# A hybrid decoder layer on one core: two queues issue the first weight loads, and the gates' columns are cast one place later

## The chip, the cores and the metric

The kernel runs on one core of one Trainium2 chip. The metric is the device time of one execution in microseconds (us); less is better. Before the change the median of three runs is 477.52 us (477.06 to 477.61). The core has a matrix engine (PE), a vector engine (DVE), a scalar engine (ACT), a general engine (POOL) and a small engine (SP) that here only issues transfers (DMAs). Every engine works off its own queue of instructions in order. PE accumulates in a small memory (PSUM); the others work in the on-chip memory (SBUF).

## The reference

One layer of a decoder trunk, on 256 tokens of width 1024, in float32:

```
proj = x @ w_in + b_in          # columns: q,k,v,o,i,f of the mLSTM; q,k,v of the attention; two gates
y_a  = sigmoid(o) * head_norm(mlstm_chunkwise(silu(conv(q)), silu(conv(k)), v, i, f))
y_b  = moba_attention(q_b, k_b, v_b, rel_bias)
mix  = (sigmoid(g_a) * (y_a @ w_a) + sigmoid(g_b) * (y_b @ w_b)) @ w_out
x    = layer_norm(ALPHA * x + mix)
x    = layer_norm(ALPHA * x + (silu(g) * up) @ w_down)      # g, up = conv(x @ w_up)
```

The change touches only how the first product begins: `x @ w_in` for the 1024 columns of `o` and the eight columns of the gates `i` and `f`.

## The kernel before

All weights lie in DRAM as a stack `wst` of chunks of 128 partitions by 2048 numbers (1 MB each), in the order in which PE uses them. Each matrix is held as a sum of two rounded parts: ACT casts a piece of the raw float32 weights to the high part (`wh`, line 94), DVE subtracts it from the raw piece and writes the low part (`wl`, line 95), and PE multiplies three times (high by high, high by low, low by high). The helper for such a pair is `split_into`. The input `x` comes transposed (`xraw`) and is split in the same way (`xth`, `xtl`).

The first four chunks make up the columns of `o`, and they are treated apart from the rest (lines 236 to 284). The inner dimension of 1024 is cut into eight steps k of 128 rows. For every k three groups of columns are needed:

- Columns 0 to 511 come from chunks 0 and 1, which are laid out by rows: a piece is 128 x 512 numbers, 256 KB, the widest. Steps 0 to 3 are in `raw` buffer 0 (`raw_105`), steps 4 to 7 in buffer 1 (`raw_106`). Their split goes to `wh_107`/`wl_108` and, for steps 4 to 7, to the borrowed buffers `yah`/`yal`.
- Columns 512 to 767 are chunk 2, whose raw buffer is the borrowed tile `sgb`; its split is `wh_109`/`wl_110`. A piece is 128 x 256 (128 KB), from step 4 on two steps together (256 KB).
- Columns 768 to 1023 are chunk 3, raw buffer `sigo`, split in `wh_111`/`wl_112`, with pieces like those of chunk 2. The eight columns of the gates (`wif`, 32 KB, loaded by POOL's queue) are split into the last eight of each step's 264 columns, so PE's products of this group need them too.

One loop (lines 246 to 259) issues all these loads on SP's queue, step by step: `xraw` first, then for steps 0 and 1 the order chunk 2, chunk 3, `raw`, later chunk 2, `raw`, chunk 3. After step 3 two small loads follow (`sga`, the biases' row, and `bif`). A second loop (lines 266 to 282) casts and subtracts in nearly the same order: `xraw`, chunk 2, (step 0: the gates' columns `wif`), chunk 3 and `raw` for steps 0 and 1. `step_o` (from line 419) then multiplies, step by step, into six accumulators: `ps_o2a`/`ps_o2b` (chunk 2, two halves of the tokens), `ps_o3a`/`ps_o3b` (chunk 3 and the gates) and `ps_o0a`/`ps_o0b` (the 512 columns). Steps 0 and 1 go in the order o2, o3, o0, the later ones o2, o0, o3. Ahead of it PE runs eight multiplications of zeros, `warm_ps` (line 211).

Every DMA from SP's or ACT's queue signals its landing on one of eight semaphores, named DMAHW0 to DMAHW7 here and called lanes below. The eight are dealt out in turn, and a DMA on a lane waits until the one before it on that lane has landed. Before the change the ninth DMA thus waits for the first, and so on. Which lane a load has is read from the cast that waits for it.

After the four chunks the rest of the program follows in `chunk_order`: for each of four groups the projections `qm`, `qb`, `km`, `kb`, `vm`, `vb`, `ga`, `gb`, then `wa`, `wb`, `wo`, the `up` and `dn` parts of the MLP. Their loads (line 89) come behind the first loop on SP's queue.

Of the kernel before, what the change touches and what calls it, by code (L numbers as in the profile page):

```python
# [21 lines left out]
KT = D // P  # L22
# [50 lines left out]
class Kernel:  # L73
# [115 lines left out]
    def run(self):  # L189
        tc, nc, ctx = self.tc, self.nc, self.ctx  # L190
# [45 lines left out]
        raw = [self.stream.tile([P, 2048], F32, tag="raw", name=f"raw{s}", bufs=3) for s in range(2)]  # L236
# [6 lines left out]
        dma = nc.sync.dma_start  # L243
        cut = [(k // 4, slice(k % 4 * 512, k % 4 * 512 + 512)) for k in range(KT)]
        pieces = {0: 1, 1: 1, 2: 1, 3: 1, 4: 2, 6: 2}
        for k, (s, c) in enumerate(cut):
            dma(xraw[:, k], self.xt_d[:, k])
            for t in (2, 3, s) if k < 2 else (2, s, 3):
                if t == s:
                    dma(raw[s][:, c], self.wst[s, :, c])  # L250
                elif k in pieces:
                    d = slice(k * 256, (k + pieces[k]) * 256)
                    dma(raw[t][:, d], self.wst[t, :, d])
                if t == 3 and k == 0:
                    nc.gpsimd.dma_start(self.wif, self.wif_d)
            if k == 3:

                dma(brow.rearrange("p (a d) -> p a d", a=2), self.rows_d[0:2, :].unsqueeze(0))
                dma(bif, self.bif_d.to_broadcast([P, 8]))
# [5 lines left out]
        v3 = [t.rearrange("p (k f) -> p k f", k=KT) for t in whl[3]]  # L265
        for k, (s, c) in enumerate(cut):
            self.split_into(xth[:, k], xtl[:, k], xraw[:, k])
            if k == 0:
                nc.gpsimd.tensor_copy(self.xfirst, xth[:, 0, 0:P])
            n = pieces.get(k, 0)  # L270
            d = slice(k * 256, (k + n) * 256)
            if n:
                self.split_into(whl[2][0][:, d], whl[2][1][:, d], raw[2][:, d])
            if k >= 2:
                self.split_into(whl[s][0][:, c], whl[s][1][:, c], raw[s][:, c])
            if k == 0:
                self.split_into(v3[0][:, :, 256:264], v3[1][:, :, 256:264], self.wif)
            if n:
                self.split_into(*(t[:, k:k + n, 0:256] for t in v3),
                                raw[3][:, d].rearrange("p (k f) -> p k f", k=n))  # L280
            if k < 2:
                self.split_into(whl[s][0][:, c], whl[s][1][:, c], raw[s][:, c])

# [1076 lines left out]
```

## Time and profile before

| | us |
|---|---|
| median of 3 runs | 477.52 |
| the profiled execution, its own time | 477.09 |
| its span, first to last instruction | 475.4 |
| PE busy in the span | 467.9 |
| DVE busy | 369.1 |
| ACT busy | 311.4 |
| POOL busy | 37.8 |

The profiled execution spends 1.7 us of its time outside the span. All views count microseconds from the start of the span. A row of the timeline has start, duration, engine, line, operation, output and inputs, shape, the count, and in brackets how long the engine sat idle before and what ended that. SPq, ACTq and POOLq are the queues that issue; the duration of a DMA there is that of its issue, not of the transfer. The view of the DMAs lists issues by line, count, size and the time from the start of the issue to the landing, which I call the flight. Line 247 issues `xraw`, 253 the pieces of chunks 2 and 3, 250 those of `raw`.

### The profile page before, as it was taken

The page shows a single profiled execution, that of the slowest core. Times are in us where ns is not written, and L with a number is a line of the kernel's source. Part 1 is how long each engine was busy: PE and PEld are TensorE (multiplying, and loading weights), DVE is VectorE, ACT ScalarE, POOL GpSimd, SP SyncE. Part 2 cuts the span into 40 slices and gives each one's busy share as a digit, 9 for nine tenths or more (in the row PEclk, how much of TensorE's full clock was granted, in tenths as well). Part 3 has the DMA queues.
Part 4 walks back from the last instruction along what each step waited for, and adds up shares of the span by engine and source line. Part 5 has one row for each costly group of instructions (what it writes and reads, how often), then busy time and mean ns, then how long its engine had stood idle before and what let it go on. Part 6 is the DMA issues. An engine that isn't in the chain of part 4 may idle for free.

```text
span 475.4 us, 9500 instructions
## 1 busy us (share of the span) xinstructions
PE 467.9 (98%) x3776; PEld 452.8 (95%) x3776; DVE 369.1 (78%) x649; ACT 311.4 (66%) x544; POOL 37.8 (8%) x73
## 2 busy tenths in 40 slices
PE   8999999999999999999999999999999999999994
PEld 6999999999999999999999999999999989999984
DVE  4786979787778778887685798788887775878876
ACT  6679878677868777968563533676555444556871
POOL 0414711000200020000100001000000000000000
PEclk9999999999999999999999999999999999999998
DMA  7995667934893577466966472874456545565202
GB/s 234 296 331 190 214 227 235 327 110 185 246 306 115 189 235 256 169 209 198 373 228 256 148 295 81 301 240 178 171 206 223 199 176 183 187 214 215 90 0 89
DMA packets 31758, 98.92 MB, mean 208 GB/s; under 512 B 11845, under 2 KB 18129, under 8 KB 22497
## 3 DMA queue, kind: packets, MB, share of 16 engines
q1 hardware_dynamic: 30482, 94.08, 56.8%
q0 software_dynamic: 1232, 4.24, 2.8%
q8 instruction: 29, 0.48, 0.4%
q14 instruction: 15, 0.12, 0.1%
HBM read 94.10 MB, written 4.21 MB: 207 GB/s over the span
## 4 chain that ended last, share of the span: by engine, by line
PE 97%; DMA 1%; DVE 0%; SPq 0%; ACT 0%; DVEq 0%; issue 0%; ACTq 0%
PE ps_up L148 25%; PE ffn L148 13%; PE mix L148 5%; PE ps_ga L148 5%; PE ps_kb L148 5%; PE ps_vm L148 5%; PE ps_vb L148 5%; PE ps_gb L148 5%; PE ps_wb L148 5%; PE ps_qm L148 5%; PE ps_km L148 5%; PE ps_qb L148 5%; PE ps_wa L148 4%; PE ps_o0a L437 1%; PE ps_o0b L437 1%; PE psn L148 1%
## 5 line engine op out<-in xcount | busy, mean ns | idle before, releaser
L95 DVE TENSOR_TENSOR wl<-raw,wh 128x1024 fp32r<-128x1024 f32 (+4 forms) x147 | 180.0, 1261 | 28.7 <-ACT wh L94 26.9
L94 ACT CAST wh<-raw 128x1024 fp32r<-128x1024 f32 (+4 forms) x147 | 151.9, 1078 | 12.3 <-DMA raw<-in_wst_dram 3.8
L148 PE MATMUL ps_up<-x1h,wl 128*128 128x256 f32 x320 | 88.4, 276 | 0.0
L148 PE MATMUL ps_up<-x1l,wh 128*128 128x256 f32 x320 | 88.4, 276 | 0.0
L148 PE MATMUL ps_up<-x1h,wh 128*128 128x256 f32 x320 | 88.4, 276 | 0.0
L148 PEld LDWEIGHTS ps_up<-x1l,wh 128*128 128x128 f32 x320 | 60.1, 188 | 0.3
L148 PEld LDWEIGHTS ps_up<-x1h,wh 128*128 128x128 f32 x320 | 60.1, 188 | 0.3
L148 PEld LDWEIGHTS ps_up<-x1h,wl 128*128 128x128 f32 x320 | 60.1, 188 | 0.0
L1131 DVE SCALAR_TENSOR_TENSOR cu<-ps_up,vec,cu 128x255 f32<-128x255 f32 (+1 forms) x80 | 33.1, 476 | 17.3 <-ACT cu L1127 17.3
L148 PE MATMUL ffn<-wh,hl 128*128 128x512 f32 (+2 forms) x94 | 35.5, 378 | 0.0
L148 PE MATMUL ffn<-wl,hh 128*128 128x512 f32 (+2 forms) x94 | 35.4, 377 | 0.0
L94 ACT CAST hh<-cu 128x256 fp32r<-128x256 f32 x22 | 8.9, 407 | 40.3 <-DVE cu L1142 40.3
L148 PE MATMUL ffn<-wh,hh 128*128 128x512 f32 (+2 forms) x94 | 35.3, 375 | 0.0
L1127 ACT ACTIVATE cu<-ps_up,vec 128x256 f32<-128x256 f32 x40 | 16.7, 469 | 17.2 <-PE ps_up L148 17.2
L148 PEld LDWEIGHTS ffn<-wh,hl 128*128 128x128 f32 x94 | 17.7, 188 | 3.2
L148 PEld LDWEIGHTS ffn<-wl,hh 128*128 128x128 f32 x94 | 17.7, 188 | 3.1
L148 PEld LDWEIGHTS ffn<-wh,hh 128*128 128x128 f32 x94 | 17.7, 188 | 3.1
L1022 POOL TENSOR_TENSOR rs<-rs,mhalf 128x1 f32<-128x1 f32 x3 | 2.1, 701 | 229.9 <-DVE rs L1021 229.9
L148 PE MATMUL ps_ga<-xth,wh 128*128 128x256 f32 x64 | 18.0, 281 | 0.0
L148 PE MATMUL mix<-wh,mgh 128*128 128x256 f32 x64 | 17.9, 279 | 0.0
L148 PE MATMUL mix<-wl,mgh 128*128 128x256 f32 x64 | 17.8, 278 | 0.0
L148 PE MATMUL ps_kb<-xth,wl 128*128 128x256 f32 x64 | 17.7, 277 | 0.0
(348 smaller groups left out, 1475.3 us busy)
## 6 DMA issues: line engine op xcount, KB each, us to landing
raw<-in_wst_dram SPq DMA_DIRECT2D x72, 1024.0 KB, 4.9
raw<-in_wst_dram SPq DMA_DIRECT2D x10, 512.0 KB, 6.5
raw<-in_wst_dram SPq DMA_DIRECT2D x8, 256.0 KB, 4.6
lnrow<-in_rows_dram POOLq DMA_DIRECT2D x4, 512.0 KB, 6.8
flip<-turn SPq DMA_DIRECT2D x8, 192.0 KB, 2.1
lg<-flip SPq DMA_DIRECT2D x32, 48.0 KB, 4.8
xraw<-in_xt_dram SPq DMA_DIRECT2D x8, 128.0 KB, 4.5
toe<-table POOLq DMA_DIRECT2D x4, 256.0 KB, 4.2
```

The source lines that it names most:

```text
L94: self.nc.scalar.copy(wh, raw)
L95: self.nc.vector.tensor_sub(wl, raw, wh.bitcast(F32))
L148: self.nc.tensor.matmul(ps, a[i], b[i], start=start and i == 0, stop=stop and i == 2)
L437: mm(ps[t], x[:, k, t * P:(t + 1) * P], w, start=start and k == 0, stop=stop and k == KT - 1)
L1022: nc.gpsimd.tensor_tensor(st["rs"], st["rs"], self.mhalf[:, 0:1], op=ALU.pow)
L1127: act.activation(cu[:, j, :], ps[:, j, :], AF.Copy, scale=tap(2, j))
L1131: v.scalar_tensor_tensor(cu[:, j, o:], ps[:, j, :S - o], tap(t, j), cu[:, j, o:], op0=ALU.mult, op1=ALU.add)
```

## The change

The eight pieces of `raw`, and the first piece of chunk 2, are issued by ACT's queue and no longer by SP's. A new inner function `rows(k)` issues piece k. Piece 0 is issued in the first loop, so at the very front of ACT's queue, together with the first piece of chunk 2. Piece k + 1 is issued in the second loop, right behind the cast of `xraw` of step k. The gates' columns are split behind chunk 3's first piece and not ahead of it.

```
         cut = [...]
         pieces = {0: 1, 1: 1, 2: 1, 3: 1, 4: 2, 6: 2}
+        def rows(k):
+            if k < KT:
+                s, c = cut[k]
+                nc.scalar.dma_start(raw[s][:, c], self.wst[s, :, c])
+
         for k, (s, c) in enumerate(cut):
             dma(xraw[:, k], self.xt_d[:, k])
-            for t in (2, 3, s) if k < 2 else (2, s, 3):
+            for t in (2, s, 3):
                 if t == s:
-                    dma(raw[s][:, c], self.wst[s, :, c])
+                    if k == 0:
+                        rows(k)
                 elif k in pieces:
                     d = slice(k * 256, (k + pieces[k]) * 256)
-                    dma(raw[t][:, d], self.wst[t, :, d])
+                    q = nc.scalar.dma_start if (t, k) == (2, 0) else dma
+                    q(raw[t][:, d], self.wst[t, :, d])
...
             self.split_into(xth[:, k], xtl[:, k], xraw[:, k])
+            rows(k + 1)
...
-            if k == 0:
-                self.split_into(v3[0][:, :, 256:264], v3[1][:, :, 256:264], self.wif)
             if n:
                 self.split_into(*(t[:, k:k + n, 0:256] for t in v3), ...)
+            if k == 0:
+                self.split_into(v3[0][:, :, 256:264], v3[1][:, :, 256:264], self.wif)
             if k < 2:
                 self.split_into(whl[s][0][:, c], whl[s][1][:, c], raw[s][:, c])
```

The front of ACT's queue before, up to the cast of `xraw` of step 1 (a `CAST` row is the high part of a split; in brackets the lane it waits for; DMASW0 is the lane of `wif`):

```order
L94 ACT_TABLE_LOAD
L94 CAST xth<-xraw 128x256 [waits DMAHW0_49]
L94 CAST wh_109<-sgb 128x256 [waits DMAHW1_49]
L94 CAST wh_111<-wif 128x8x8 [waits DMASW0_49]
L94 CAST wh_111<-sigo 128x256 [waits DMAHW2_49]
L94 CAST wh_107<-raw_105 128x512 [waits DMAHW3_49]
L94 CAST xth<-xraw 128x256 [waits DMAHW4_49]
```

The same place now, up to the third piece of `raw`:

```order
L261 DMA sgb<-in_wst_dram 128x256
L250 DMA raw_105<-in_wst_dram 128x512
L94 ACT_TABLE_LOAD
L94 CAST xth<-xraw 128x256 [waits DMAHW1_49]
L250 DMA raw_105<-in_wst_dram 128x512 [waits DMAHW2_49]
L94 CAST wh_109<-sgb 128x256 [waits DMAHW0_49]
L94 CAST wh_111<-sigo 128x256 [waits DMAHW3_49]
L94 CAST wh_111<-wif 128x8x8 [waits DMASW0_49]
L94 CAST wh_107<-raw_105 128x512
L94 CAST xth<-xraw 128x256 [waits DMAHW4_49]
L250 DMA raw_105<-in_wst_dram 128x512 [waits DMAHW7_49]
```

Two issues now stand ahead of the table load, and piece 1 of `raw` stands ahead of the first cast of chunk 2. The lanes of step 0 are 0 (`sgb`), 1 (`xraw`), 2 (`raw` piece 0) and 3 (`sigo`): the cast of piece 0 needs no wait of its own, since the issue of piece 1, four rows ahead of it, has waited for lane 2 already.

SP's queue before, from its eighth issue on:

```order
L250 DMA raw_105<-in_wst_dram 128x512
L247 DMA xraw<-in_xt_dram 128x256 [waits DMAHW0_49]
L253 DMA sgb<-in_wst_dram 128x256 [waits DMAHW1_49]
L250 DMA raw_105<-in_wst_dram 128x512 [waits DMAHW2_49]
L253 DMA sigo<-in_wst_dram 128x256 [waits DMAHW3_49]
L247 DMA xraw<-in_xt_dram 128x256 [waits DMAHW4_49]
```

SP's queue now, from its sixth issue on:

```order
L253 DMA xraw<-in_xt_dram 128x256
L261 DMA sgb<-in_wst_dram 128x256 [waits DMAHW0_49]
L261 DMA sigo<-in_wst_dram 128x256 [waits DMAHW1_49]
L253 DMA xraw<-in_xt_dram 128x256 [waits DMAHW3_49]
L261 DMA sgb<-in_wst_dram 128x256 [waits DMAHW4_49]
L261 DMA sigo<-in_wst_dram 128x256 [waits DMAHW5_49]
```

The pieces of `raw` are gone from SP's queue, so the pieces of chunks 2 and 3 and of `xraw` follow each other directly, and the load of step 2's chunk 2 waits for the first piece of chunk 2. PE's instructions, and DVE's but for the swapped gates' columns, stand in the same order as before.

## Prediction
> **What bounds the kernel now.** I read the page first: engines, then the chain that ended last.
>
> ```profile
> span 475.4 us, 9500 instructions
> PE 467.9 (98%) x3776; PEld 452.8 (95%) x3776; DVE 369.1 (78%) x649; ACT 311.4 (66%) x544; POOL 37.8 (8%) x73
> PE 97%; DMA 1%; DVE 0%; SPq 0%; ACT 0%; DVEq 0%; issue 0%; ACTq 0%
> ```
>
> PE is the chain: 97% of the span. What stands in the chain besides PE is short, and the change touches one piece of it, the start. So I look at the chain in its first 9 us (start, duration, what).
>
> ```profile
> 0.81 0.37 SPq L247
> 1.23 0.43 SPq L253
> 1.71 0.42 SPq L253
> 2.17 3.91 DMA raw<-in_wst_dram
> 6.09 0.02 issue
> 6.11 0.63 ACT wh L94
> 6.78 0.50 PE ps_o0a L437
> ```
>
> The chain begins with the first three issues on SP, then the flight of the first wide piece (`raw` piece 0): issued at 2.17, landed at 6.08, cast at 6.11, multiplied from 6.78. The timeline shows what PE does around it.
>
> ```profile
> 0.85 3.57 PE L211 MATMUL warm_ps<-const-float32-0.0 128*128 128x512 bf16 x8 [0.85 <-PEq L1349]
> ...
> 4.27 0.43 PE L437 MATMUL ps_o2a<-wh,xth 128*128 128x256 f32 x1
> 4.54 0.28 PE L437 MATMUL ps_o2b<-wh,xth 128*128 128x256 f32 x1
> ...
> 5.95 0.29 PE L437 MATMUL ps_o3b<-wl,xth 128*128 128x264 f32 x1
> 6.78 0.50 PE L437 MATMUL ps_o0a<-wh,xth 128*128 128x512 f32 x1 [0.55 <-ACT wh L94]
> ...
> 8.27 0.28 PE L437 MATMUL ps_o2a<-wh,xth 128*128 128x256 f32 x1
> ...
> 11.06 0.28 PE L437 MATMUL ps_o2a<-wh,xth 128*128 128x256 f32 x1
> ```
>
> Step 0 takes PE from 4.27 to 8.27, 4.00 us. Step 1, 8.27 to 11.06, takes 2.79 us and has no gap. Of the 1.21 us between them, 0.15 is the restart of the first product (the second follows after 0.27 and not after 0.12, the spacing of steady products of this width) and stays; **1.06 us is what an undisturbed step 0 would save**. After 6.78 PE never waits: the chain goes on as PE alone, and the first projection starts at 28.09.
>
> ```profile
> 28.09 5.44 PE ps_qm L148 x48
> 33.54 5.44 PE ps_qb L148 x48
> ```
>
> From there block follows block without a gap, so a shift of the start arrives at the end whole, and nothing behind it takes it up.
>
> **The change part by part.** The first product needs the cast of chunk 2's first piece. Before, ACT and SP did this:
>
> ```profile
> 0.81 1.28 ACT L94 ACT_TABLE_LOAD   x1 [0.81 <-PEq L1349]
> 3.22 0.41 ACT L94 CAST xth<-xraw 128x256 fp32r<-128x256 f32 x1 [1.13 <-DMA xraw<-in_xt_dram]
> 3.81 0.41 ACT L94 CAST wh<-sgb 128x256 fp32r<-128x256 f32 x1 [0.19 <-DMA sgb<-in_wst_dram]
> 4.51 0.25 ACT L94 CAST wh<-wif 128x64 fp32r<-128x64 f32 x1 [0.29 <-DMA wif<-in_wif_dram]
> 4.77 0.41 ACT L94 CAST wh<-sigo 128x256 fp32r<-128x256 f32 x1
> ...
> 2.17 0.44 SPq L250 DMA_DIRECT2D raw<-in_wst_dram  x1
> 6.10 0.33 SPq L253 DMA_DIRECT2D sigo<-in_wst_dram  x1
> ```
>
> Now piece 1 of `raw` is issued by ACT ahead of that cast, and it waits for lane 2, that is for the landing of piece 0. ACT's queue is in order. So **everything behind that issue waits for piece 0 as well**: the casts of chunk 2, chunk 3, the gates and `raw` of step 0, thus DVE's subtractions and PE's first product. A wait that held only the last third of step 0 now holds all of it.
>
> The sum, with L for the landing of piece 0: the issue starts 0.03 behind L (as the cast does before, 6.08 to 6.11), takes 0.33 (SP's issues with a wait ahead of them; ACT has issued no DMA before, so its price is taken from there, bounds 0.33 and 0.44), and the first product follows 0.46 behind the start of the cast (3.81 to 4.27). First product: L + 0.82. Once it starts, the other operands of step 0 are there: the casts of chunk 3, gates and `raw` follow each other at some 0.3 to 0.5 us, ahead of PE's groups. So the 1.06 is saved, and the shift is L + 0.82 - 4.27 - 1.06 = **L - 4.51**. It is zero if piece 0 lands at 4.51, that is 1.57 earlier than before.
>
> How early does it land? Issued second on ACT, at the earliest at 1.23, where SP's second issue stood, instead of 2.17. With the same flight it lands at 5.1, a shift of +0.6. If nothing is gained it lands at 6.1, +1.6. The wider ends: the flight of the half as large first piece of chunk 2 from 1.23 (3.8, a shift of -0.7), and the longest flight of a wide piece in this loop from 2.17 (8.3, +3.8).
>
> ```profile
> sgb<-in_wst_dram SPq DMA_DIRECT2D x1, 128.0 KB, 2.6
> sigo<-in_wst_dram SPq DMA_DIRECT2D x1, 128.0 KB, 3.0
> DMA to landing us min/median/max: 3.9/4.6/6.1
> ```
>
> (The last row is of line 250 alone.) Between them the stretches decide (the last two columns are the DMA engines' busy share and GB/s):
>
> ```profile
> 2.00:3.00 1.00, 1.00 (x4) 0.37 (x3) 0.00 (x0) 0.09 (x1) 0.08 (x1) 1.00 0.80 214
> 3.00:4.00 1.00, 1.00 (x4) 0.24 (x2) 0.34 (x1) 0.59 (x2) 0.00 (x0) 1.00 0.89 252
> 4.00:5.00 1.00, 1.00 (x6) 0.73 (x6) 0.72 (x3) 0.69 (x3) 0.00 (x0) 1.00 0.88 156
> 5.00:6.00 1.00, 1.00 (x9) 0.85 (x7) 0.44 (x2) 0.18 (x1) 0.00 (x0) 1.00 0.95 300
> ```
>
> The DMA engines are 0.80 to 0.95 busy from 2 us on, so it is the transfers and not the issues that take the time, and piece 0 now shares them with the pieces that SP issues meanwhile. I credit half of the 0.94 us of the earlier issue: L = 5.6, **a shift of +1.1 us**.
>
> The Trainium skill, page "DMA: Bandwidth & Descriptors", section "Issuing engines are not separate DMA queues", says that transfers issued by several engines run on the same 16 DMA engines and interleave, which saves the sequencer's issue time alone. The busy shares above agree; by that rule the shift lies toward +1.6, by the issue times alone it would be +0.6.
>
> The other edits. The table load moves behind two issues of about 0.42, to 1.65 to 2.93, and the landing of `xraw` at 3.2 hides it; without that cover it costs what it is late. The gates' cast behind chunk 3's: nothing, since chunk 3's piece was issued at 1.71 with a flight of 3.0, so it landed at 4.7, and its cast at 4.77 did not wait for the gates' cast; both sides within 0.25, that cast's length. Seven more issues on ACT, 0.33 to 0.44 each: 2.3 to 3.1 us in some 18 us, against casts of 1.8 us per step of 2.79; PE's 2.79 hide them. SP loses nine issues and runs ahead; chunk 3's piece of steps 4 and 5, which came latest before PE's need, then comes earlier:
>
> ```profile
> 17.47 0.62 ACT L94 CAST wh<-sigo 128x512 fp32r<-128x512 f32 x1 [1.11 <-DMA sigo<-in_wst_dram]
> 18.74 0.28 PE L437 MATMUL ps_o3a<-wh,xth 128*128 128x264 f32 x1
> ```
>
> The cast ends at 18.09 and PE needs it by 18.74 at the latest, so this was tight, but it held nothing up, and there is nothing to win.
>
> Against its own time the sum is 477.09 + 1.1 = 478.2. That execution lies 0.43 under the median of the runs shown (477.52); the prediction is for a median, **478.6 us**.
>
> **The rivals.**
>
> *Piece 0 lands early (not slower).* Issued side by side with nothing else wide in flight, it flies like chunk 2's first piece: L = 3.8, the shift -0.7, **476.9**. It decides at L = 4.51. For it: the flight of 3.9 includes the queue of three pieces ahead. Against: twice the bytes, and the busy shares. Chance 0.20.
>
> *The queues take turns.* ACT's issues fall between SP's, piece 0 is issued at 2.17 as before and lands at 6.1: +1.6, **479.1**. The change then does not do what it says, and only the wait is left. For it: SP's issues are 0.43 back to back and 0.33 after a wait, as if something behind them set the pace. No run here shows ACT issuing. Chance 0.16. The Trainium skill, same page, section "Queues, rings and completion order", says that SP and ACT have rings of their own but no descriptor generator of their own; that is this case.
>
> *PE runs slowly after the longer pause.* The eight products of zeros take 3.57 us, 0.45 each, where products of the same 512 columns later follow each other after 0.23:
>
> ```profile
> 7.35 0.40 PE L437 MATMUL ps_o0a<-wh,xtl 128*128 128x512 f32 x1
> 7.58 0.40 PE L437 MATMUL ps_o0b<-wh,xtl 128*128 128x512 f32 x1
> ```
>
> The PEclk column reads 1.00 in both, so only the spacing tells. Now PE pauses from 4.42 to 6.4. If it falls back for a stretch of 3.57 at half the pace, that costs 1.8 more: **480.4**. Against: the pause of 0.55 before did nothing, and 2.0 is still short of 3.57. Chance 0.10. The Trainium skill, page "TensorE: Matmul & The Clock Gate", section "What's actually happening", states half the clock until a window of 3413 ns was busy; the spacing agrees, and no run here shows what 2 us of pause do.
>
> *ACT's own loop sets the pace.* A piece of `raw` is issued only behind the next step's `xraw` cast, which stands behind the cast of the piece before. From a landing to the issue two pieces later lie some 1.1 us of casts; with the flight that must fit in two steps, 5.58 us, so flights up to about 4.4 are hidden. Before they were 3.9 to 6.1. At 5.0, piece 1 is 0.4 late (it must land 4.6 behind L) and each of two further rounds 0.6: 1.6 more, **480.2**. Against: ACT's queue holds at most two pieces. Chance 0.12.
>
> **How the numbers follow.** The forecast has 0.42, from +0.6 to +1.6 around 478.6. A measurement of this kernel tells about 0.2% (0.95 us) from no change, so the bound is 478.47; of the forecast I put 0.24 above it and 0.18 below. Slower: 0.24 + 0.16 + 0.10 + 0.12 = 0.62. Faster by that much would need L under 3.56, below the early rival's 3.8: 0.04 of its 0.20. The same: 0.18 + 0.16 = 0.34. The range, 477.1 to 480.6, takes in all but half of the early rival and the worst of the last two.
>
> **What would show it.** ACT's third issue starting within 0.1 us of piece 0's landing, and chunk 2's first cast behind it, not at 3.8: the wait is real. The first product at L + 0.8, then step 0 in about 2.9 us without the gap at 6.2: the 1.06 is saved. The first projection at 29.2 instead of 28.09: the sum. A spacing of 0.2 in the first products of 256 columns would be the slow pace; gaps ahead of `ps_o0a` in steps 1, 3 or 5 ACT's loop. I am wrong if that cast starts before piece 0 has landed, or if the piece lands before 4.5.

## The result and the profile after

The changed kernel takes 480.45 us in the median of eight runs (479.2 to 483.8), the kernel before 477.35 in eight runs beside it (477.06 to 478.23). The ratio is 1.0073, with an interval from 1.006 to 1.0087: slower by 3.1 us. The forecast was 478.6, slower by 1.1; the direction was right and the size was not.

The profiled execution of the changed kernel took 481.24 us, 4.15 more than the one of before (477.09). Its page, with the span, the busy times and the engines' shares of the chain:

```profile
span 479.5 us, 9500 instructions
...
PE 468.5 (98%) x3776; PEld 452.7 (94%) x3776; DVE 368.7 (77%) x649; ACT 310.0 (65%) x544; POOL 36.2 (8%) x73
...
PE 93%; DMA 5%; ACT 1%; DVE 0%; ACTq 0%; DVEq 0%; issue 0%
```

PE is busy for 468.5 us, almost as before (467.9), while the span grew by 4.1: PE waits more. The transfers' share of the chain went from 1% to 5%. The chain of waits of the changed kernel, cut to its first 35 us (start, duration, what), shows for whom it waits:

```profile
0.80 0.41 ACTq L261
...
1.24 4.07 DMA raw<-in_wst_dram
...
5.33 0.33 ACTq L250
...
5.70 1.38 ACT wh L94 x4
...
7.27 3.74 DMA raw<-in_wst_dram
...
11.04 5.87 DMA raw<-in_wst_dram
...
17.29 8.97 DMA raw<-in_wst_dram
...
26.28 0.63 ACT yah L94
...
26.95 0.50 PE ps_o0a L446
```

The first rows are the forecast's path: piece 0 of `raw` is issued at 1.24 and lands at 5.30, the third issue starts 0.03 behind that, and only then come the casts. The row at 17.29 is a second delay, not in the forecast's sum: piece 6 of `raw` flies 8.97 us, and step 6 waits for it. The rows between show why it was issued only then: ACT issues piece 2 at 7.27, piece 4 at 11.04, when piece 2 has landed, and piece 6 at 17.29, when piece 4 has landed (16.91) and its cast has begun. PE's timeline of the changed kernel, the first product of steps 0 to 3 and the one that waits in step 6:

```profile
6.16 0.39 PE L446 MATMUL ps_o2a<-wh,xth 128*128 128x256 f32 x1 [1.75 <-ACT wh L94]
...
9.08 0.28 PE L446 MATMUL ps_o2a<-wh,xth 128*128 128x256 f32 x1
...
11.91 0.28 PE L446 MATMUL ps_o2a<-wh,xth 128*128 128x256 f32 x1
...
15.39 0.28 PE L446 MATMUL ps_o2a<-wh,xth 128*128 128x256 f32 x1
...
26.95 0.50 PE L446 MATMUL ps_o0a<-yah,xth 128*128 128x512 f32 x1 [2.28 <-ACT yah L94]
```

Step 1 starts at 9.08 instead of 8.27 (+0.81). Step 2, from 11.91 to 15.39, takes 3.48 us instead of 2.79 (+0.69). In step 6 PE stands still for 2.28 us, and the step takes 5.36 instead of 2.84 (+2.5). Together 4.0, which is the growth of the span. So three delays have to be explained, and only the first was in the forecast.

### The profile page after: what moved, and what is told of

It reads as the page before. It is cut to its first block, busy times and chain, and to the rows that moved or that the text cites. A ratio compares the mean times of both kernels' runs of the same rounds, so it can differ in the third digit from the quotient of the medians.

```text
span 479.5 us, 9500 instructions
## 1 busy us (share of the span) xinstructions
PE 468.5 (98%) x3776; PEld 452.7 (94%) x3776; DVE 368.7 (77%) x649; ACT 310.0 (65%) x544; POOL 36.2 (8%) x73
## 4 chain that ended last, share of the span: by engine, by line
PE 93%; DMA 5%; ACT 1%; DVE 0%; ACTq 0%; DVEq 0%; issue 0%
PE ps_up L148 25%; PE ffn L148 13%; DMA raw<-in_wst_dram 5%; PE mix L148 5%; PE ps_ga L148 5%; PE ps_kb L148 5%; PE ps_vm L148 5%; PE ps_vb L148 5%; PE ps_gb L148 5%; PE ps_wb L148 5%; PE ps_qm L148 5%; PE ps_km L148 5%; PE ps_qb L148 5%; PE ps_wa L148 4%; PE psn L148 1%; PE pss L148 1%
```

## Experiments

Each ratio below is against runs of the kernel before, made beside it on the same chip; the medians of these were between 476.91 and 477.14. "Step k" starts with its first product of `ps_o2a`.

**Delay in step 6: the next chunk's loads.** In the changed kernel SP has nothing of `raw` left to issue, and it reaches the loads of the next chunk (line 89, two of 512 KB) earlier. SP's timeline of the changed kernel:

```profile
16.25 1.35 SPq L89 DMA_DIRECT2D raw<-in_wst_dram  x2
```

The same queue of the kernel before, with piece 6 and the next chunk:

```profile
14.21 0.43 SPq L250 DMA_DIRECT2D raw<-in_wst_dram  x1
...
17.84 1.01 SPq L89 DMA_DIRECT2D raw<-in_wst_dram  x2
```

Before, piece 6 went out at 14.21, and the megabyte of the next chunk behind it. Now the first half of that megabyte goes out at 16.25 and the second at 17.27, and piece 6 only at 17.29, from ACT. Two shifts turned the order round: SP reaches the next chunk 1.59 us earlier, and ACT issues piece 6 3.08 us later than SP did. The theory: the next chunk's bytes lie ahead of it. Three runs test that, from both sides. In the first, ACT issues the next chunk behind piece 7:

```diff
             rows(k + 1)
+            if k == KT - 2:
+                self.load(4, nc.scalar)
```

> The changed kernel, but the two loads of the next chunk (512 KB each, line 89) are issued by ACT right behind the last piece of raw, and no longer by SP ahead of pieces 6 and 7. Theory (two costs: step 0 behind the lane wait, +0.8; piece 6 behind the next chunk's 1 MB, +2.3 in the profiled run): the flight of piece 6 falls from 9.0 to under 6 us, the gap of 2.3 ahead of step 6's o0 products is gone, the first product stays at about 6.2; median 478.0 to 478.6, some 2.2 under the changed kernel and 0.8 over the one before. Rival (piece 6 is late because ACT issues it late, at 17.3 instead of 14.2, whatever SP does): flight and gap stay within 0.5 us, median about 480.4. Rival (ACT's queue is served worse by the DMA engines): flight over 7 us, median above 479.5.

Measured: 480.11 (ratio 1.0067, 1.0053 to 1.008). In ACT's timeline of this run piece 6 is still issued late, and yet it is there in time:

```profile
16.91 0.35 ACTq L250 DMA_DIRECT2D raw<-in_wst_dram  x1
...
22.08 0.62 ACT L94 CAST yah<-raw 128x512 fp32r<-128x512 f32 x1 [0.68 <-DMA raw<-in_wst_dram]
```

Its cast starts 5.17 us behind its issue, not 9, and there is no gap in step 6. So the late issue alone does no harm. The time hardly moved, because step 2 became longer (4.16 us) and a new gap of 0.38 came up in the first projection. The part on the gap was right, the expected time was not.

The second run goes the other way round: the kernel before, every load on SP, but the next chunk ahead of pieces 6 and 7.

```diff
                 if t == s:
-                    dma(raw[s][:, c], self.wst[s, :, c])
+                    if k < 6:
+                        dma(raw[s][:, c], self.wst[s, :, c])
...
+        self.load(4)
+        for s, c in cut[6:]:
+            dma(raw[s][:, c], self.wst[s, :, c])
```

> The kernel before, all loads on SP, but the next chunk's two loads of 512 KB are issued ahead of pieces 6 and 7 of raw. Theory (a piece that stands behind 1 MB of the next chunk lands late, whoever issues it): flight of piece 6 of 7 us or more (6.0 before), pieces 6 and 7 late, a gap of 1 to 3 us ahead of step 6's or 7's o0 products, median 478.5 to 480.5. Rival (the delay needs ACT's late issue or ACT's queue): no gap over 0.3 us, median within 0.5 of the kernel before.

Measured: 479.34 (1.0054, 1.0038 to 1.0069). PE's timeline of this run:

```profile
25.27 0.50 PE L441 MATMUL ps_o0a<-yah,xth 128*128 128x512 f32 x1 [1.85 <-ACT yah L94]
```

The same product waits, with no load on ACT at all. Piece 6 is issued at 17.78 here and flies 6.8 us, a little less than the 7 expected. The third run takes the changed kernel and gives pieces 6 and 7 back to SP:

```diff
-            if k < KT:                                  # in rows(k)
+            if k < 6:
...
+                    if k >= 6:
+                        dma(raw[s][:, c], self.wst[s, :, c])
```

> The changed kernel, but SP issues pieces 6 and 7 of `raw`, each in its old place behind the chunks of its k and so ahead of the next chunk's loads. Theory (the gap ahead of step 6 comes of 1 MB of the next chunk issued ahead of these two pieces): piece 6 flies 6 us or less and lands before 22, no gap ahead of step 6, step 2 still 3.5 us, the time 480.45 - 2.55 = 477.9 within 0.4. Rival (ACT's queue is served late whatever SP issues, pieces 2 to 5 included): pieces 4 or 5 make a gap instead, and the time stays over 479.5.

Measured: 479.35 (1.0051, 1.0037 to 1.0066), no gap in step 6; piece 6 goes out at 15.06 and flies 4.3 us. So a piece 6 that is issued late and has the megabyte ahead of it makes the gap, whoever issues it. But 479.35 is not the 477.9 expected, and in its profile step 0 took 4.15 us, step 2 only 2.78. Something else had come up in step 0.

**Delay in step 2: DVE beside POOL.** In the changed kernel DVE's row for a piece of chunk 2, normally 0.42 us, and for one of `raw`, normally 0.69, are much longer between 11 and 14 us:

```profile
10.73 0.42 DVE L95 TENSOR_TENSOR xtl<-xraw,xth 128x256 fp32r<-128x256 f32 x1
11.06 1.39 DVE L95 TENSOR_TENSOR wl<-sgb,wh 128x256 fp32r<-128x256 f32 x1
12.38 1.65 DVE L95 TENSOR_TENSOR wl<-raw,wh 128x512 fp32r<-128x512 f32 x1
13.95 0.50 DVE L95 TENSOR_TENSOR wl<-sigo,wh 128x256 fp32r<-128x256 f32 x1
```

POOL in the same kernel, at the same time:

```profile
11.01 1.30 POOL L268 PARTITION_BROADCAST bo<-sga  x1 [8.94 <-DMA sga<-in_rows_dram]
12.19 1.42 POOL L269 PARTITION_BROADCAST bvm<-sga  x1
```

Each of the two subtractions takes nearly 1 us more (1.39 for 0.42, 1.65 for 0.69) while POOL copies a bias row to all partitions. DVE's timeline of the kernel before:

```profile
10.12 0.42 DVE L95 TENSOR_TENSOR wl<-sgb,wh 128x256 fp32r<-128x256 f32 x1
...
12.70 1.26 DVE L95 TENSOR_TENSOR wl<-raw,wh 128x512 fp32r<-128x512 f32 x1 [0.31 <-ACT wh L94]
13.88 1.38 DVE L95 TENSOR_TENSOR wl<-sigo,wh 128x256 fp32r<-128x256 f32 x1
```

POOL's first broadcast there:

```profile
12.09 1.47 POOL L260 PARTITION_BROADCAST bo<-sga  x1 [10.00 <-DMA sga<-in_rows_dram]
```

SP's issue of the biases' row `sga`, which the broadcast waits for, in the kernel before:

```profile
8.90 0.32 SPq L258 DMA_DIRECT2D sga<-in_rows_dram  x1
```

The same issue in the changed kernel:

```profile
7.03 0.33 SPq L266 DMA_DIRECT2D sga<-in_rows_dram  x1
```

The slowdown is old, but it met rows of step 3, which PE multiplied only at 15.46 and 16.40. Now it meets rows of step 2. In step 2 DVE is some 1 us ahead of PE in both kernels: before, chunk 2's row ended at 10.54 for a product at 11.53; now, at its normal length, it would end at 11.48 for a product due at 12.39. What moved is the broadcasts. They wait for `sga`, which SP issued at 8.90 before and issues at 7.03 now, and they start 1.08 us earlier, while PE's step 2 starts 0.85 later. So the theory is: the same slowdown now falls where DVE's lead is too short to pay it from. First the two broadcasts were held back behind the last cast of `x`, in the changed kernel and in the run with the next chunk behind:

```diff
-        nc.gpsimd.partition_broadcast(bo, ...); (self.bvm, ...)
...
+        nc.gpsimd.tensor_copy(bo[:, 0:8], xth[:, 7, 0:8])     # waits for the cast
+        nc.gpsimd.partition_broadcast(bo, ...); (self.bvm, ...)
         self.step_o(whl, bo)
```

> The changed kernel, but POOL's two broadcasts of the bias rows wait until the last chunk of x is cast (about 20 us); every load is issued as in the changed kernel. Theory (DVE is slowed while POOL broadcasts, and step 2 waits for DVE): DVE's rows between 11 and 14 us go back from 1.39 and 1.65 to 0.42 and 0.69 us, step 2 takes 2.8 us in place of 3.48, and slow DVE rows show up beside the broadcasts at their new place. The time stays at 480.4 within 0.4, since piece 6 of `raw` lands at 26.3 us whatever step 2 does, so the gap ahead of step 6 grows from 2.3 to 3.0 us. Rival 1 (step 2 waits for late data): DVE's rows may be short but step 2 stays at 3.5. Rival 2 (the two delays add): 479.7.

> The run that put the next chunk's loads behind piece 7 (480.11), and POOL's two broadcasts behind the last cast of x as well. Theory: its step 2 goes from 4.16 to 2.8 us, nothing is late afterwards but the 0.38 us gap in the first projection: 480.1 - 1.4 = 478.7 within 0.4. Rival (late data in step 2, or DVE is slowed at the new place as much): 479.8 to 480.3.

Measured: 485.16 (1.0179, 1.0154 to 1.0204) and 482.85 (1.0131, 1.011 to 1.0152). DVE's timeline of the first of them:

```profile
11.16 0.42 DVE L95 TENSOR_TENSOR wl<-sgb,wh 128x256 fp32r<-128x256 f32 x1
11.75 0.69 DVE L95 TENSOR_TENSOR wl<-raw,wh 128x512 fp32r<-128x512 f32 x1 [0.17 <-ACT wh L94]
```

The rows are short again, and step 2 takes 2.78 and 2.79 us in the two runs. That fits, but it does not show the cause yet: step 0 took 4.65 and 4.43 us in these two, and a slow step 0 alone gives DVE time (in the run with pieces 6 and 7 on SP the rows are long, and yet step 2 took 2.78). The pair of runs that shows it comes below. The expected times failed, since the late broadcasts cost more elsewhere: POOL started them only at 31.14 in the second run, its fill of the gates' tile stands behind them, DVE waited 3.27 us for that fill, and the weights' subtractions behind it came too late for `ps_qb` (a gap of 1.59 at 38.6). Why POOL started that late, no view shows. In the first run the gap in step 6 shrank to 1.16 us instead of growing to 3.0, since its step 0 was slow.

**Step 0: PE's clock.** The slow step 0 is in no term of the sum, but a slow PE after the pause is one of the rivals. PE's timeline of the run with pieces 6 and 7 on SP, the change of pace on the way:

```profile
7.63 0.29 PE L448 MATMUL ps_o3a<-wl,xth 128*128 128x264 f32 x1
...
7.94 0.63 PE L448 MATMUL ps_o0a<-wh,xth 128*128 128x512 f32 x1
8.37 0.63 PE L448 MATMUL ps_o0b<-wh,xth 128*128 128x512 f32 x1
...
11.30 0.28 PE L448 MATMUL ps_o2a<-wl,xth 128*128 128x256 f32 x1
```

Products of 512 columns follow each other after 0.43 us where 0.23 is usual. The table by stretches of the same run has the granted clock (1.00 is PE's full clock) as its third column from the right:

```profile
7.60:7.80 0.20, 0.20 (x4) 0.20 (x3) 0.20 (x1) 0.20 (x1) 0.00 (x0) 0.99 1.03 266
7.80:8.00 0.20, 0.20 (x3) 0.20 (x3) 0.20 (x2) 0.20 (x2) 0.00 (x0) 0.50 0.96 225
11.00:11.20 0.20, 0.20 (x3) 0.20 (x3) 0.20 (x2) 0.00 (x0) 0.20 (x1) 0.50 0.67 191
11.20:11.40 0.20, 0.20 (x3) 0.20 (x3) 0.20 (x1) 0.00 (x0) 0.20 (x1) 0.98 0.72 200
```

From 7.8 to 11.2 us, 3.4 us, PE runs at half the clock, 1.45 us after a pause of 1.94 (4.42 to 6.35) had ended. The profiled execution of the changed kernel had a pause of 1.75 and no such stretch. Two edits on this run, each alone and both together, tell the costs apart: the pause is filled with four more products of zeros, and the broadcasts are replaced by zeros, which leaves the bias rows out of the result. The last run takes the broadcasts out of the kernel before:

```diff
-        for i in range(8):                                  # products of zeros
+        for i in range(12):
...
-        nc.gpsimd.partition_broadcast(bo, ...); (self.bvm, ...)
+        nc.gpsimd.memset(bo, 0.0); nc.gpsimd.memset(self.bvm, 0.0)
```

> The run with pieces 6 and 7 on SP (479.35), and twelve products of zeros ahead in place of eight, so that PE works through the pause from 4.4 to 6.2 us. Theory (in that run the pause made PE's clock fall back to one half from 7.8 to 11.2 us, which cost 1.2 us in step 0, while DVE's delay beside POOL's broadcasts sits in its shade): step 0 takes 2.9 us in place of 4.15, but step 2 now waits for DVE, 3.5 to 4.2 us in place of 2.8, so that the time hardly moves: 478.4 to 479.3. Rival (the pace alone is the rest): step 2 stays at 2.8 and the time is 478.0.

> The run with pieces 6 and 7 on SP, eight products of zeros, and POOL fills the two bias tiles with zeros at the start in place of its two broadcasts (the bias rows are left out of the sums). Theory: DVE's rows between 10 and 15 us are 0.42 and 0.69 us throughout and no step waits for DVE; what is left depends on PE's pace in step 0: 477.9 where it is the fast one (2.9 us), up to 479.2 where it is the slow one (4.2 us); the median between, with a spread of over 1 us. Rival (DVE alone is the rest): 477.9 with a narrow spread.

> Both: twelve products of zeros, zeros in place of the two broadcasts, pieces 6 and 7 on SP. Theory (four costs and no other: 0.8 us of lane wait, DVE beside POOL, PE's pace after the pause, the next chunk ahead of piece 6): step 0 at 6.2, all steps at 2.8 to 2.9, the first projection at 28.9, 477.9 within 0.3, and the narrow spread of the kernel before. Rival (another cost is hidden behind these): over 478.4, with a gap at a new place.

> The kernel before with zeros in place of POOL's two broadcasts (the bias rows are left out of the sums). Theory: DVE's rows at 12.7 and 13.9 us go from 1.26 and 1.38 to 0.69 and 0.42 us, but no product waited for them, so 477.1 within 0.3: the broadcasts cost nothing where the casts run ahead of PE by enough. Rival (the broadcasts cost the kernel before something as well): 476.5 or less.

| kernel | median, range | ratio to before, interval | step 0 | step 1 | step 2 |
|---|---|---|---|---|---|
| pieces 6, 7 on SP | 479.35 (478.5 to 480.57) | 1.0051 (1.0037 to 1.0066) | 4.15 | 3.12 | 2.78 |
| and twelve products | 479.55 (479.29 to 479.77) | 1.005 (1.0035 to 1.0065) | 2.92 | 3.25 | 3.58 |
| and no broadcasts | 479.1 (477.66 to 480.76) | 1.0044 (1.0027 to 1.0061) | 4.46 | 2.80 | 2.79 |
| and both | 478.2 (478.0 to 478.87) | 1.0021 (1.001 to 1.0033) | 2.95 | 2.78 | 2.79 |
| before, no broadcasts | 476.8 (476.48 to 477.67) | 0.9995 (0.9986 to 1.0005) | 4.37 | 2.79 | 2.78 |

Neither edit alone gains anything that can be measured; both together gain 1.1 us. Rows two and four are the pair that shows DVE beside POOL as a cause: step 0 is fast in both, and without the broadcasts steps 1 and 2 go from 3.25 and 3.58 to 2.78 and 2.79, and the median falls by 1.35 us. Rows three and four show the clock: without broadcasts, the filled pause takes step 0 from 4.46 to 2.95, and the median falls by 0.9, though their intervals overlap. The two delays lie side by side: where PE is slow in step 0, DVE has the time to catch up, and where PE is fast, it waits for DVE in steps 1 and 2. The spread of over 2 us in rows one and three shrinks to under 1 where the pause is filled. A clock that falls back in some executions only would do that, but the runs are few, and the kernel before spread over 2.2 us beside them. In the kernel before, removing the broadcasts changes nothing that can be measured. PE's timeline of the run with both:

```profile
6.42 0.38 PE L448 MATMUL ps_o2a<-wh,xth 128*128 128x256 f32 x1 [1.02 <-ACT wh L94]
...
9.37 0.28 PE L448 MATMUL ps_o2a<-wh,xth 128*128 128x256 f32 x1
...
12.15 0.28 PE L448 MATMUL ps_o2a<-wh,xth 128*128 128x256 f32 x1
...
14.94 0.28 PE L448 MATMUL ps_o2a<-wh,xth 128*128 128x256 f32 x1
```

Step 1 starts 1.10 behind that of before (8.27), and from there on every step is like that of before. So the start costs 1.10 us here, the forecast's own term. The median is 1.2 us above that of before. This profiled execution, 478.87, was the slowest of its eight; it waits another 0.45 us at 276.88, in the product `mix`, and what the others have there is not shown.

**The wait ahead of chunk 2's cast.** Three runs move the place of ACT's issues. In the first, pieces 0 and 1 go out at ACT's front, and piece k + 2 behind all casts of step k:

```diff
-                    if k == 0:
+                    if k < 2:
                         rows(k)
...
-            rows(k + 1)                  # behind the cast of xraw
...
+            rows(k + 2)                  # behind the last cast of step k
```

> The changed kernel, but pieces 0 and 1 of raw are both issued at the front of ACT's queue and every later piece k + 2 stands behind all casts of step k, so no issue that waits stands ahead of a cast of its own step. The next chunk's loads stay with SP. Theory (two costs): the first product starts 1.5 to 2 us earlier than in the changed kernel, at 4.2 to 4.6, and step 1 begins at 8.3 or earlier (9.1 changed, 8.3 before); the gap ahead of step 6 stays at 1.5 us or more, since pieces 6 and 7 still stand behind the next chunk's loads; median about 479.3 to 480.3. Rival (the late start is the engines' or the DMA's, not the lane wait): first product still after 5.8, step 1 at 9.0 or later.

Measured: 479.0 (1.005, 1.0031 to 1.0069). The first product starts at 4.26, so the wait is gone, but the third issue now waits for its lane until 8.0 ahead of step 1's casts, and step 1 starts at 9.15. The wait had moved from step 0 to step 1. The gap expected in step 6 did not come: ACT issues piece 6 at 17.95 here and SP the next chunk at 17.99, and the cast of piece 6 starts 5.44 us behind its issue. In the second, ACT issues only the two loads at its front and SP all others, as in the kernel before:

```diff
+                q = nc.scalar.dma_start if k == 0 and t != 3 else dma
                 if t == s:
-                    dma(raw[s][:, c], self.wst[s, :, c])
+                    q(raw[s][:, c], self.wst[s, :, c])      # so too for chunk 2
```

> The kernel before, but the first piece of chunk 2 and piece 0 of raw are issued by ACT at the front of its queue; all else as before, no issue of ACT's waits. Theory: two queues issue the first four loads at once, piece 0 lands at about 5.3 (6.1 before), the gap of 0.55 ahead of step 0's o0 products shrinks to about 0.1 or goes, step 1 begins at 7.5 to 8.0 (8.3 before), median 0.3 to 0.8 us under the kernel before: 476.6 to 477.1. Rival (the queues take turns or the engines are full, so nothing lands earlier): step 1 at 8.2 to 8.4, median 477.4.

Measured: 477.18 (1.0004, 0.9995 to 1.0012), no change. The first product starts at 4.08, but the gates' columns land later than before, their cast starts at 5.68 instead of 4.51, and PE waits 0.64 for them; step 1 starts at 8.49. The third run takes the one with pieces 6 and 7 on SP and zeros for the broadcasts, and issues piece k + 1 behind all casts of step k:

> The run with pieces 6 and 7 on SP and zeros in place of POOL's two broadcasts, eight products of zeros, and each of ACT's issues moved from behind the cast of x to the end of its step's casts, so that no cast of step 0 stands behind the wait for a lane. Theory (the last 1.1 us are that wait alone): chunk 2's first cast at 3.7, first product at 4.2 as before, no pause of PE over 0.7 us and so one spell of slow pace, step 1 at 8.3 to 8.6, the first projection at 28.0 to 28.3, 477.0 to 477.4. Rival (issuing from ACT costs something of its own): a later step waits for a piece of `raw`, and the time is 478 or more.

Measured: 489.79 (1.0266, 1.0251 to 1.0281). The first product starts at 4.07 and step 1 at 8.09, as expected without the wait; then the rival came, and far worse than thought. The chain of this run:

```profile
6.25 4.14 DMA raw<-in_wst_dram
10.41 5.00 DMA raw<-in_wst_dram
15.45 4.12 DMA raw<-in_wst_dram
19.60 7.27 DMA raw<-in_wst_dram
26.89 5.56 DMA raw<-in_wst_dram
```

Piece k + 1 is issued only when piece k has landed and its cast has begun, so one flight of 4 to 7 us follows the other, where a step of PE takes 2.8. This run does not show what the wait alone is worth in the end; the steps of the run with both edits do.

**Small ones.** The gates' cast alone was moved in the kernel before:

> The kernel before with the gates' columns' cast moved behind the fourth chunk's piece and nothing else. Theory: costs and wins nothing, 477.1 within 0.3; the cast of the gates' columns takes 0.25 us and moves behind one of 0.41 us that waits for nothing, and the third product group of step 0 needs both. Rival: the move itself is part of the 3.1 us lost, then 477.5 or more.

Measured: 477.08 (1.0001, 0.9991 to 1.0011): it costs nothing. And a try at a version better than both, the two loads at ACT's front and the gates' columns as its third issue:

```diff
+                    if k == 0:
+                        q(self.wif, self.wif_d)      # no longer on POOL's queue
```

> A try at a version that beats both: the run with the two first pieces alone at ACT's front (477.18), with the gates' columns as third issue there in place of POOL's queue, since step 0 waited 0.64 us for their cast at 5.68. Theory: the gates' columns land before 5.2, the gap ahead of chunk 3's products shrinks to 0.2 or less, step 1 at 8.0 to 8.2 in place of 8.5, the time 0.2 to 0.4 below that run: 476.7 to 477.0. Rival (the slow pace of PE up to some 5.4 us and the landing of piece 0 set step 1, whatever comes between): 477.1 to 477.3.

Measured: 477.74 (1.0022, 1.0009 to 1.0035). The gates' columns came later still (their cast at 6.11), and the gap ahead of chunk 3's products grew to 1.46. No version here beats the kernel before.

## Why the prediction was right in direction and wrong in size

1. **The wait for piece 0 is real and sized right.** ACT's third issue starts 0.03 behind the landing, the first product 0.86 behind it (0.82 in the sum), and step 0 runs in 2.92 without the gap. The sum was L - 4.51; with L = 5.30 (5.6 was taken) it gives +0.79, and step 1 starts 0.81 later. With the other costs taken away, 1.2 us stay by the medians and 1.10 at the start of step 1, where the forecast had 1.1.
2. **The step that failed: "SP loses nine issues and runs ahead", with "there is nothing to win".** I looked for what SP's lead may gain, and put what it sends out early at nothing. It sends out the next chunk's megabyte 1.59 us earlier, and with piece 6 issued 3.08 us later by ACT that puts the megabyte ahead of it. The flight of piece 6 grew from 6.0 us (issue at 14.21, cast at 20.21) to 8.97. In the profiled execution that costs 2.5 us. By the medians, giving pieces 6 and 7 back to SP takes 1.1 off (480.45 to 479.35), and putting the megabyte behind them takes 0.3 off (480.11), with new delays in both. One reason for the difference is that piece 6's landing hardly depends on PE: what holds PE up in steps 0 to 2 shortens the gap in step 6. In the first run with late broadcasts the cast of piece 6 starts at 26.39, as good as in the changed kernel (26.28), and the gap is 1.16.
3. **"Nothing behind it takes it up" failed too, the other way.** The sum let a late step 0 run on at full speed. But SP's lead also brings the two broadcasts of POOL 1.08 us forward, and PE's step 2 comes 0.85 later, so they are felt in step 2: +0.69 in the profiled execution. That they cost time behind a fast step 0 is shown by the pair of runs with twelve products; that their earlier start is what made them felt is read from the rows, and no run moves their start alone.
4. **The rivals.** The early landing did not come: 5.30 against 4.51. The queues do not take turns: ACT's first two issues start at 0.80 and 1.24, beside SP's at 0.81 and 1.24. ACT's own loop was half right. It did not make gaps in steps 1, 3 or 5, but it runs through pieces 0, 2 and 4 to piece 6, and issues that at 17.29 for 14.21. Alone that is harmless, as the run with the next chunk behind piece 7 shows; the gap needs the megabyte ahead as well. The run that issues behind the casts shows how it looks when the loop does set the pace. The slow PE after the pause was not in the profiled execution of the changed kernel, nor in that with the next chunk behind piece 7 (pauses of 1.75 and 1.90 us), but in four others with pauses of 1.80 to 2.24 us it was, with a step 0 of 4.15 to 4.65 us. In two of these the granted clock fell to 0.50 after some products at the full pace; in the two with late broadcasts the products were slow from the first one on, while the view shows a clock of 1.00. The Trainium skill, page "TensorE: Matmul & The Clock Gate", section "What's actually happening", says that the window of 3413 ns runs freely, and that where it lies decides when the clock changes; the stretch of 3.4 us above agrees. In how many executions of the changed kernel it falls back stays open, since only one of them has a trace.

So of the 3.1 us some 1.2 are the wait. The other 1.9 are the next chunk ahead of piece 6, DVE beside POOL, and in some executions the half clock. How they share the 1.9 is not shown, since each of them hides part of the next.

## What to carry to other kernels

When issues are moved off a queue, follow the queue that got shorter as well: ask what it now sends out early, whose bytes these overtake, and which engine starts earlier for it. An issue with a wait ahead of it stalls the engine that makes it, so it belongs behind the work that is due, but not so far that each load waits for the one before. And where one delay shades another, undo them together: here neither of two edits alone gained anything, and both did.

## What the runs showed of the hardware

- A transfer of 256 KB on ACT's queue took 8.97 us when half a megabyte had been issued on SP's queue 1.04 us before it and another half 0.02 us before; from 19 to 21 us ACT's queue moved nothing in this trace. It took about 5 when the megabyte was issued behind it. Queues of their own did not keep them apart.
- A DVE subtraction of two operands takes nearly 1 us longer while POOL broadcasts a row (0.42 to 1.39, 0.69 to 1.65), and is short again without. The Trainium skill, page "SBUF — State Buffer", section "Who interferes with whom", says that a DVE instruction with two SBUF inputs contends with a GpSimd instruction that reads SBUF; the rows agree.
- A pause of PE of 1.94 us, less than the stretch of 3.4, was followed by half the clock from 7.8 to 11.2 us; one of 1.90 in another run was not.
- A load of 32 KB moved from POOL's queue to ACT's was not there sooner in one execution of each: its cast started at 6.11 instead of 5.68.
